# Rolling a matrix by 100 columns: the two DMA rings take blocks from opposite ends instead of sharing each block

## The chip, the cores and the metric

The kernel runs on one core of a Trainium2 chip. The metric is device time in microseconds, the median of several runs; smaller is better. A core has compute engines, of which only GpSimd (POOL in the profile) and VectorE (DVE) do anything here, and 16 DMA engines that move data between the main memory (HBM) and the on-chip memory (SBUF), or from HBM to HBM. Instruction queues of SP, ACT and GpSimd issue the transfers. The transfers of SP and ACT go through one ring each; each transfer is cut into packets that are spread over the 16 DMA engines.

## The reference

x is a matrix of 8192 x 8192 float32 values, 268.44 MB; a row is 32 KiB. The output is x with every row rolled to the right by `shift` = 100 columns:

```python
def reference(x: np.ndarray, shift: int) -> np.ndarray:
    return np.roll(x, shift, axis=1)
```

So output column 100 + i is input column i, and output columns 0 to 99 are input columns 8092 to 8191. There is no arithmetic: 268.44 MB are read and 268.44 MB written.

## The kernel before

With s = 100, the kernel splits the output's columns at a = 128, the next multiple of 128.

Columns 128 to 8191 (the body, 32,256 bytes of each row) are copied from HBM to HBM by line 41, without a stop in SBUF. The rows are grouped in 128 blocks of 64 rows, 2 MiB each. A row's number is 64c + 4e + j, with c the block, e from 0 to 15 and j from 0 to 3. One transfer takes one j of one block: 16 rows, four rows apart, 504 KB. Its 16 rows become 16 packets of 32,256 bytes, one for each DMA engine, and each engine closes with a packet of 4 bytes that counts up the transfer's semaphore. The loop runs over the blocks upwards; j = 0 and j = 2 are issued by SP, j = 1 and j = 3 by ACT (`engines[j % 2]`). So both rings share each block. In the last four blocks each transfer is cut in two at column `mid` = 4096, into 248 KB and 256 KB. Each ring has 264 transfers in all. The Tile framework gives each ring four semaphores in turn, and an issue waits until the transfer that used its semaphore before has landed.

Columns 0 to 127 (the head) come behind this in the program and are GpSimd's: in 16 stages of 512 rows it loads the wrapped columns and the first 28 columns of the rows into SBUF (lines 70, 71 and 74), VectorE copies them together (lines 72 and 75), and line 78 writes them out, 512 bytes a row. These transfers go through GpSimd's own queue (q0 in the profile).

Line 47 and what stands around it (a > 512) isn't reached with this shift. No order is set by hand other than that of the loops, and no body transfer depends on another or on the heads.

Of the kernel before, what the change touches and what calls it, by code (L numbers as in the profile page):

```python
# [1 line left out]

# [4 lines left out]


@with_exitstack
def kernel(  # L10
    ctx: ExitStack,
    tc: tile.TileContext,
    x: bass.AP,
    shift: int,
    out: bass.AP,
):
    nc = tc.nc
    n_rows, n_cols = x.shape
    s = shift % n_cols
    a = -(-s // 128) * 128  # L20
    g = a - s
    P = nc.NUM_PARTITIONS
    engines = [nc.sync, nc.scalar]
    n_chunks = 16
    rows = n_rows // n_chunks

    xm = x.rearrange("(c e j) w -> c j e w", e=16, j=4)
    om = out.rearrange("(c e j) w -> c j e w", e=16, j=4)
    if a < n_cols:
        blocks = n_rows // 64
        mid = (a + n_cols) // 256 * 128
        for c in range(blocks):
            parts = ((a, mid), (mid, n_cols)) if c >= blocks - 4 and a < mid else ((a, n_cols),)
            for j in range(4):
                for lo, hi in parts:  # L40
                    engines[j % 2].dma_start(out=om[c, j, :, lo:hi], in_=xm[c, j, :, lo - s:hi - s])
    if a == 0:
        return


    if a > 512:
        for i in range(n_chunks):
            r = slice(i * rows, (i + 1) * rows)
            nc.gpsimd.dma_start(out=out[r, :s], in_=x[r, n_cols - s:])
            if g > 0:  # L50
                nc.gpsimd.dma_start(out=out[r, s:a], in_=x[r, :g])
        return

    Q = 4
    n_st = n_rows // (P * Q)
    reads = ctx.enter_context(tc.tile_pool(name="reads", bufs=n_st))  # L60
    heads = ctx.enter_context(tc.tile_pool(name="heads", bufs=n_st))
    xt = x.rearrange("(k p q) c -> k p q c", q=Q, p=P)
    ot = out.rearrange("(k p q) c -> k p q c", q=Q, p=P)
    tiles = []
    for k in range(n_st):
        t = reads.tile([P, Q - 1, a], x.dtype)
        h = heads.tile([P, Q, a], x.dtype)
        lead = bass.AP(tensor=x.tensor, offset=(k * P * Q + 1) * n_cols - s,
                       ap=[[Q * n_cols, P], [n_cols, Q - 1], [1, a]])
        nc.gpsimd.dma_start(out=t[:], in_=lead, single_packet=True)  # L70
        nc.gpsimd.dma_start(out=h[:, Q - 1, :s], in_=xt[k, :, Q - 1, n_cols - s:], single_packet=True)  # L71
        nc.vector.tensor_copy(h[:, :Q - 1, :s], t[:, :, :s])  # L72
        if g > 0:
            nc.gpsimd.dma_start(out=h[:, 0, s:], in_=xt[k, :, 0, :g], single_packet=True)  # L74
            nc.vector.tensor_copy(h[:, 1:, s:], t[:, :, s:])  # L75
        tiles.append(h)
    for k, h in enumerate(tiles):
        nc.gpsimd.dma_start(out=ot[k, :, :, :a], in_=h[:], single_packet=True)  # L78


# [1 line left out]
_INS = ['x', 'shift']  # L82
_OUTS = [((8192, 8192), 'float32')]

_NUMBERS = {'shift': 100}


# [26 lines left out]
```

## Time and profile before

| | |
|---|---|
| time, median of 3 runs | 829.13 us (828.62 to 831.27) |
| the profiled execution: its span, first to last instruction | 818.3 us; the page gives no time of its own around the span, and the median lies 10.8 us above it |
| VectorE, GpSimd busy | 7.8 us, 41.1 us |
| the two rings' 31.5 KB packets and completions, share of 16 DMA engines | 48.2% and 46.1% |
| GpSimd's queue | 4.7% |
| moved by all queues | 272.71 MB, mean 333 GB/s |

In the page, a queue's row has its packets, its megabytes and the time that its packets took as a share of the span of 16 engines. GB/s counts each byte that a DMA engine moves once; a copy from HBM to HBM reads and writes it, and so loads HBM twice. The rows of 40 digits or numbers are 40 equal slices of the span, 20.5 us each; a 9 for DMA means that the engines were busy for 90% of the slice or more. A row of DMA issues has the issuing queue, the number of issues, the size of each and the median time from issue to landing.

### The profile page before, as it was taken

How to read it: one execution, taken by the hardware profiler on the slowest of the kernel's cores; microseconds unless marked ns; L12 is line 12 of the kernel's file. 1: busy time of each engine (PE TensorE's matmuls, PEld its weight loads, DVE VectorE, ACT ScalarE, POOL GpSimd, SP SyncE). 2: the span in 40 equal slices, each digit the busy share in tenths (PEclk: the TensorE clock that was granted, in tenths of full speed). 3: DMA queues.
4: the chain of work that ended last, by engine and by line, in shares of the span. 5: the costliest groups of instructions: out<-in, count | busy, mean ns of one | idle time of the engine just before them, and what ended most of it. 6: DMA issues, size and time to landing. Idle time of an engine off the chain costs nothing. (4 is left out here: it accounts for less than half of the span.)

```text
span 818.3 us, 689 instructions
## 1 busy us (share of the span) xinstructions
DVE 7.8 (1%) x32; POOL 41.1 (5%) x68
## 2 busy tenths in 40 slices
DVE  0000000000000000000000000000000000000000
POOL 3011111111010000000000000000000000000000
DMA  9999999999999999999999999999999999999998
GB/s 304 340 344 338 341 334 345 341 346 350 353 352 357 347 332 321 335 328 326 333 330 323 330 331 330 331 326 333 330 328 334 333 330 339 328 333 334 328 318 294
DMA packets 20229, 272.71 MB, mean 333 GB/s; under 512 B 9472, under 2 KB 9728, under 8 KB 11776
## 3 DMA queue, kind: packets, MB, share of 16 engines
q1 hardware_dynamic: 8448, 132.14, 48.2%
q10 hardware_dynamic: 8448, 132.14, 46.1%
q0 software_dynamic: 3328, 8.39, 4.7%
q14 instruction: 5, 0.04, 0.0%
HBM read 268.44 MB, written 268.44 MB: 656 GB/s over the span
## 5 line engine op out<-in xcount | busy, mean ns | idle before, releaser
L78 POOL DMA_DIRECT2D out_dram<-h x16 | 11.4, 712 | 87.2 <-DMA out_dram<-h 51.7
L70 POOL DMA_DIRECT2D t<-in_x_dram x16 | 12.1, 759 | 32.1 <-DMA h<-in_x_dram 31.3
L74 POOL DMA_DIRECT2D h<-in_x_dram x16 | 8.6, 538 | 85.7 <-DMA t<-in_x_dram 85.7
L71 POOL DMA_DIRECT2D h<-in_x_dram x16 | 8.9, 558 | 23.9 <-DMA h<-in_x_dram 23.9
L72 DVE COPY h<-t 128x300 f32<-128x300 f32 x16 | 5.9, 368 | 190.4 <-DMA t<-in_x_dram 190.4
L75 DVE COPY h<-t 128x84 f32<-128x84 f32 x16 | 3.2, 201 | 0.0
L95 POOL MEMSET const-float32-0.0<- 128x1 f32 x1 | 0.1, 99 | 0.2 <-issue 0.2
L95 POOL MEMSET const-bfloat16-1.0<- 128x1 bf16 x1 | 0.1, 101 | 0.0
L95 POOL MEMSET const-uint8-127<- 128x1 uint8 x1 | 0.1, 99 | 0.0
L95 POOL MEMSET const-float32-1.0<- 128x1 f32 x1 | 0.1, 98 | 0.0
## 6 DMA issues: line engine op xcount, KB each, us to landing
out_dram<-in_x_dram ACTq DMA_DIRECT2D x248, 504.0 KB, 12.5
out_dram<-in_x_dram SPq DMA_DIRECT2D x248, 504.0 KB, 12.5
out_dram<-h POOLq DMA_DIRECT2D x16, 256.0 KB, 63.0
t<-in_x_dram POOLq DMA_DIRECT2D x16, 192.0 KB, 32.6
out_dram<-in_x_dram SPq DMA_DIRECT2D x8, 256.0 KB, 5.9
out_dram<-in_x_dram ACTq DMA_DIRECT2D x8, 256.0 KB, 5.8
out_dram<-in_x_dram SPq DMA_DIRECT2D x8, 248.0 KB, 6.1
out_dram<-in_x_dram ACTq DMA_DIRECT2D x8, 248.0 KB, 6.1
```

Of the source, the lines that this page charges most:

```text
L70: nc.gpsimd.dma_start(out=t[:], in_=lead, single_packet=True)
L71: nc.gpsimd.dma_start(out=h[:, Q - 1, :s], in_=xt[k, :, Q - 1, n_cols - s:], single_packet=True)
L72: nc.vector.tensor_copy(h[:, :Q - 1, :s], t[:, :, :s])
L74: nc.gpsimd.dma_start(out=h[:, 0, s:], in_=xt[k, :, 0, :g], single_packet=True)
L75: nc.vector.tensor_copy(h[:, 1:, s:], t[:, :, s:])
L78: nc.gpsimd.dma_start(out=ot[k, :, :, :a], in_=h[:], single_packet=True)
L95: nc = _bacc.Bacc("TRN2", target_bir_lowering=False, num_devices=1)
```

## The change

The loop over the blocks is cut to half its length, and in each pass both rings get a block of their own: SP block c, ACT block 127 - c. Each ring now takes all four j of its block, in order. SP starts at the first block and goes upwards to block 63, ACT starts at the last and goes downwards to block 64. The transfers that are cut in two are those of the last two passes (blocks 62 and 63 for SP, 65 and 64 for ACT). The transfers themselves (rows, columns, sizes, number) are the same as before; which ring issues a transfer, and when, differs. The heads aren't changed.

```diff
         blocks = n_rows // 64
         mid = (a + n_cols) // 256 * 128
-        for c in range(blocks):
-            parts = ((a, mid), (mid, n_cols)) if c >= blocks - 4 and a < mid else ((a, n_cols),)
+        for c in range(blocks // 2):
+            last = c >= blocks // 2 - 2 and a < mid
+            parts = ((a, mid), (mid, n_cols)) if last else ((a, n_cols),)
             for j in range(4):
                 for lo, hi in parts:
-                    engines[j % 2].dma_start(out=om[c, j, :, lo:hi], in_=xm[c, j, :, lo - s:hi - s])
+                    for ring, b in zip(engines, (c, blocks - 1 - c)):
+                        ring.dma_start(out=om[b, j, :, lo:hi], in_=xm[b, j, :, lo - s:hi - s])
     if a == 0:
         return
```

## The prediction

> **What bounds the kernel now.** I read the overview of the page first, then its DMA queues, then the waits of SP's queue, and last the DMA answers for single stretches.
>
> ```profile
> span 818.3 us, 689 instructions
> DVE 7.8 (1%) x32; POOL 41.1 (5%) x68
> DMA  9999999999999999999999999999999999999998
> GB/s 304 340 344 338 341 334 345 341 346 350 353 352 357 347 332 321 335 328 326 333 330 323 330 331 330 331 326 333 330 328 334 333 330 339 328 333 334 328 318 294
> ...
> q1 hardware_dynamic: 8448, 132.14, 48.2%
> q10 hardware_dynamic: 8448, 132.14, 46.1%
> q0 software_dynamic: 3328, 8.39, 4.7%
> ...
> HBM read 268.44 MB, written 268.44 MB: 656 GB/s over the span
> ```
>
> No compute engine matters: VectorE is busy for 1% of the span and GpSimd for 5%. The 16 DMA engines are busy from the first slice to the last, and the three queues' shares add to 99.0%. So time is saved only if a packet gets shorter, and lost only if one gets longer. The page's chain of waits is of no use here: it follows GpSimd's small transfers and ends at 269 us, while the copies run on to 817 us.
>
> The two big queues are the rings of SP (q1) and ACT (q10), told apart by the semaphores of their issues. They move equal bytes in equal packets, and still SP's packets take 2.1% of the span more.
>
> ```profile
> SPq L41 <- DMA out_dram<-in_x_dram: 671.1, 260, 4.8
> ```
> ```profile
> out_dram<-in_x_dram ACTq DMA_DIRECT2D x248, 504.0 KB, 12.5
> out_dram<-in_x_dram SPq DMA_DIRECT2D x248, 504.0 KB, 12.5
> ```
>
> SP waits 671.1 us in 260 waits, each for one of its own earlier copies. It issues 264 copies on four semaphores in turn, so all but the first four wait (264 - 4 = 260): four copies of a ring are in flight, and one lands 12.5 us after its issue. The issuing is far from the limit: 264 issues of 510 ns are 135 us.
>
> The stretch in which nothing but the two rings runs, 290 to 780 us, is the one that the change is priced in:
>
> ```profile
> DMA packets 10073, 161.85 MB, mean 330 GB/s; under 512 B 5030, under 2 KB 5030, under 8 KB 5058
> ...
> q1 hardware_dynamic: 5018, 80.94, 50.5%
> q10 hardware_dynamic: 5013, 80.78, 49.1%
> ```
>
> Half of a queue's packets are 4-byte completions. A 31.5 KB packet of SP therefore takes 0.505 x 490 us x 16 / 2509 = 1.58 us, one of ACT 0.491 x 490 x 16 / 2507 = 1.54 us. The packet records of the trace show two things more. The shortest whole packets take 1.19 us, about a quarter of them do, and the longest twentieth over 2.1 us: an engine can go faster than it mostly goes, so what stretches the packets is the memory behind the engines, or their meeting in it. And most turns of an engine in this stretch read: SP's packet, ACT's packet straight behind it, then the two completions.
>
> Is that memory at a ceiling? A copy counts twice in HBM, GpSimd's transfers to and from SBUF once. By the bytes of the queues that gives, for 2 to 100, 100 to 200, 200 to 290, 290 to 535 and 535 to 780 us, 654, 660, 667, 658 and 663 GB/s. The mixture changes from 15% of GpSimd's small packets to none, and the sum stays within 2%.
>
> **The change, part by part.**
>
> *Counts and sizes: nothing.* Before, 124 blocks of four copies are whole and the last four are cut in two; after, each ring has 62 whole blocks and two cut ones. That is 264 issues a ring both times, 248 of 504 KB and 8 each of 248 and 256 KB, cut at its end. Each copy still has 16 rows, one to each of the 16 packets, spaced four rows (128 KiB) apart. Issues still alternate SP, ACT, so the four semaphores of a ring and its waits stay; what is queued behind a waiting issue is its own ring's next copy, as now. The cut copies' order changes from SP, SP, ACT, ACT to SP, ACT, SP, ACT: at most one issue earlier or later, 0.5 us, hidden by the three copies in flight. With no cover it would be those 0.5 us.
>
> *The end: nothing.* From 780 us on, the engines are 89% busy against 99 to 100% before; the halves drain there on both rings, and will again. If one ring ended ahead of the other its engines would take the other's packets without turns, so no engine would be idle for it.
>
> *GpSimd's and VectorE's work: nothing.* Their instructions come behind the copies in the program, on another queue, and touch columns 0 to 127 alone. All their waits are for their own transfers or VectorE's copies. They end at 269 us of issuing, which leaves 548 us of cover.
>
> *The addresses: the whole question.* Before, an engine's turn takes row 4e + j with SP and the next row, 4e + j + 1, with ACT: neighbours in x and in the output, and both rings are within a block or two (2 MiB each). After, the turn takes row 4e + j of block c with SP, and the same row of block 127 - c with ACT, an odd number of blocks, from 254 MiB down to 2 MiB, away. No row shows such a turn, so it is bounded from both sides by the gap between the two rings, the one place in the trace where equal packets have unequal prices. ACT's packet follows straight behind its lower neighbour and is the cheaper. If all its advantage comes from that neighbour and is lost, ACT's share rises by 2.1% of the span: 0.021 x 818.3 = 17.2 us. If none does, 0. In the other direction, SP's packets could fall to ACT's level when the rings no longer meet in a block: 17.2 us less. In the stretch of the rings alone the gap is 1.4% (50.5 against 49.1), which over the span is 11.5 us; this is the nearest row, as there the turns are undisturbed. But ACT's packet also has no completion ahead of it, which the change leaves, so I count some of the 11.5 to that and take 9 us.
>
> I choose the loss and not the gain because a gain needs room in the memory: the sum of HBM traffic never went above 667 GB/s in five long stretches, 1.7% above the mean of 656, while nothing holds it from below.
>
> *A rule against the change.* The row is the two rings' present spacing: a row or three apart, 656 GB/s in all. The Trainium skill, "DMA: Bandwidth & Descriptors", section "Latency and other measured facts", says that copies between HBM tensors slow down when the streams are a large power of two apart (207 GB/s at a pitch of 512 KiB, 164 at 2 MiB, 103 at 4 MiB), and it offers channel aliasing as an unproven reason. If the spacing of the rings, odd multiples of 2 MiB, cost all that the page gives for 2 MiB, an estimate by it would be 818.3 x 207/164 = 1033 us of span. No run here shows it.
>
> *The sum.* The page gives the span only, 818.3 us; the first instruction fetch in the packet records is 10.5 us ahead of it, together 828.8, against a median of 829.13 of the runs. So span and median agree within 0.4 us, and I count from the median: 829.1 + 0 (counts) + 0 (end) + 0 (GpSimd) + 9 (addresses) = **838 us**, 1.1% more.
>
> **The rivals.**
>
> *Nothing changes (829 us).* The memory is at its ceiling and doesn't care for order. For it speaks the sum of 654 to 667 GB/s under very different mixtures. Against it: a quarter of the packets run at 1.19 us and others at nearly twice that, so a packet does depend on what it meets, and a result within 0.3% (2.5 us, about what a measurement of this kernel can tell from no change) would need the meetings to cost exactly the same.
>
> *Faster: the rings stop meeting (812 us).* Two streams in one block of 2 MiB may meet more often in one part of the memory than streams in two distant ones. If SP's packets then cost what ACT's do, 17.2 us go: 812 us. The best slice of the late stretch, 339 GB/s against the mean of 330, gives 818.3 x (1 - 330/339) = 22 us: 807 us, the lower bound. It decides as soon as the late sum passes 667 GB/s. Against it: the best long stretch is 667.
>
> *Clearly slower: equal places collide (852 us and more).* SP's and ACT's packets in a turn, and all the engines' that are in step, stand at equal distances from the start of their blocks. If places equal but for whole blocks share a part of the memory, ACT's read starts where SP's write still drains. The lowest late slice of whole packets, 321 GB/s, is the nearest row: 818.3 x (330/321 - 1) = 23 us, 852; with both rings' packets dearer by 2.1% it is 34 us, 863. For it speaks the long tail of packets over 2.1 us, which shows that meetings happen; against it, that in the present order, too, a copy's write stands opposite its own read, 16 pairs at any time, and the sum is still 656. The page's rule named above would be this rival's cause.
>
> **How the numbers follow.** My forecast, slower by 0.3 to 2.5%, gets 0.42; clearly slower 0.17; no change 0.15; faster 0.26. Slower is thus 0.59, same 0.15, faster 0.26. The forecast alone would lie between 832 and 849. As cases of both signs hold much of the chance, the range takes the bounds of both: 807 us, with some 0.06 below it, and 863, with some 0.12 above it.
>
> **What the profile after will show.** The queues' packets and bytes must be the same, the 264 issues a ring and 12 to 13 us to landing too, and the engines' shares must still add to about 99%. If I am right, q10's share rises to at least q1's, and the stretch from 290 to 780 us moves about 326 GB/s. If shares of both rings rise together, it is the collision. If both fall and the stretch passes 333 GB/s, memory had room, and the ceiling was one of the old order alone. If the engines' shares add to clearly less than 99%, I have missed a wait. I would be wrong above all if the ceiling that I read from five stretches is no property of the memory but of the two rings' nearness, which all five have in common.

## The result: 0.35% slower, and the profile after

The changed kernel takes 832.51 us (828.60 to 836.06 in 22 runs) beside 829.68 us of the kernel before (826.53 to 831.27). The ratio is 1.0035, with a 95% interval from 1.0023 to 1.0047: a loss of 2 to 4 us, where 9 were forecast.

The page after, in the lines that answer to those of before (the overview, the DMA rates, the queues and the HBM traffic):

```profile
span 829.3 us, 689 instructions
DVE 7.8 (1%) x32; POOL 41.1 (5%) x68
...
GB/s 301 350 328 338 340 334 344 334 343 347 346 335 354 326 329 328 325 333 325 325 328 325 333 327 314 327 333 321 328 325 325 323 327 333 328 327 335 319 302 287
...
q1 hardware_dynamic: 8448, 132.14, 47.1%
q10 hardware_dynamic: 8448, 132.14, 46.7%
q0 software_dynamic: 3328, 8.39, 5.0%
...
HBM read 268.44 MB, written 268.44 MB: 647 GB/s over the span
```

Its DMA issues, and what SP's queue waited for (total us, times, longest):

```profile
out_dram<-in_x_dram ACTq DMA_DIRECT2D x248, 504.0 KB, 12.8
out_dram<-in_x_dram SPq DMA_DIRECT2D x248, 504.0 KB, 12.8
```
```profile
SPq L38 <- DMA out_dram<-in_x_dram: 681.7, 260, 5.3
```

And its stretch from 290 to 780 us:

```profile
DMA packets 9993, 160.20 MB, mean 327 GB/s; under 512 B 4976, under 2 KB 4976, under 8 KB 5033
...
q10 hardware_dynamic: 4958, 79.97, 49.9%
q1 hardware_dynamic: 4958, 79.97, 49.5%
```

Packets, bytes, waits and issues are the same in number, and the three queues still fill 98.8% of the 16 engines. So nothing waits that didn't wait before; each packet takes a little longer. The 327 GB/s of this stretch can't be set against the 330 of the page before, though.

The two pages may not be subtracted. The profiled execution of the change took 831.04 us with a span of 829.3, and in all later profiles, too, the time is 1.8 us above the span. The first page, 818.3 us, so belongs to an execution of about 820 us, faster than any of the 22 runs of before (826.53 at least). In the experiments, the unchanged kernel takes 818.25 us on one chip and 829.3 to 829.9 us on three others: the first page reads as one of a faster chip. The 11.0 us between the pages' spans are therefore mostly chip and not change. That the late stretch came out at 327 GB/s where 326 were forecast, with q10's share above q1's there, proves nothing either: experiment 5 shows the kernel before with 328 GB/s and q10 ahead on a chip of like speed. Each experiment below is compared with the kernel before on its own chip: a number like 1.0022 is its time divided by that of the kernel before, with the 95% interval behind it.

### The profile page after: what moved, and what is told of

Its sections match the earlier page's. It is cut to its first block, busy times and chain, and to the rows that moved or that the text cites. A ratio compares the mean times of both kernels' runs of the same rounds, so it can differ in the third digit from the quotient of the medians.

```text
span 829.3 us, 689 instructions
## 1 busy us (share of the span) xinstructions
DVE 7.8 (1%) x32; POOL 41.1 (5%) x68
```

## The experiments

To follow them, write an engine's packets in their order. A turn is SP's packet, then ACT's, and then comes the next turn. With each row named by its place j in its block:

- before: SP 0, ACT 1, SP 2, ACT 3, and so on, in one block
- the change: SP 0, ACT 0, SP 1, ACT 1, and so on, with ACT in a far block, at the same place as SP

Four theories could explain a loss: the *neighbour* (a turn no longer takes two adjacent rows, which is my forecast), the *distance* of the two regions, the *equal place* (two rows in a turn that lie at the same place of their 2 MiB blocks collide), and the *direction* (ACT goes downwards).

**1. Even and odd blocks, both upwards.** Near, equal places, no neighbours.

```diff
-                    for ring, b in zip(engines, (c, blocks - 1 - c)):
+                    for ring, b in zip(engines, (2 * c, 2 * c + 1)):
```

> SP takes the even blocks and ACT the odd ones, both upwards, so the rings stay 2 MiB apart at equal places of their blocks. Neighbour theory (an engine's turn on row r and r + 1 is what the change loses): 1.0035 of the time before, as in the change. Distance theory (two far regions cost): 1.000, since the rings are next to each other. Equal-place theory (rows equal but for whole blocks collide): 1.0035 or more. Direction theory (ACT going downwards costs): 1.000.

Measured: 1.0022 (1.0009 to 1.0035). Slower with the rings only 2 MiB apart and without a descending ring: against the distance and the direction as the whole cause.

**2. Two halves of the matrix, both upwards.** Far, equal places, no neighbours, nothing descends.

```diff
-                    for ring, b in zip(engines, (c, blocks - 1 - c)):
+                    for ring, b in zip(engines, (c, blocks // 2 + c)):
```

> SP takes blocks 0 to 63 and ACT blocks 64 to 127, both upwards: always 128 MiB apart at equal places. Neighbour: 1.0035. Distance: 1.0035. Equal place: 1.0035, and more if a larger power of two aliases more. Direction: 1.000.

Measured: 1.0030 (1.0018 to 1.0042). The direction is out. The constant 128 MiB cost no more than the change's odd multiples of 2 MiB.

**3. The change with ACT two rows on.** Everything as in the change but the equal place.

```diff
-                    for ring, b in zip(engines, (c, blocks - 1 - c)):
-                        ring.dma_start(out=om[b, j, :, lo:hi], in_=xm[b, j, :, lo - s:hi - s])
+                    for ring, (b, i) in zip(engines, ((c, j), (blocks - 1 - c, (j + 2) % 4))):
+                        ring.dma_start(out=om[b, i, :, lo:hi], in_=xm[b, i, :, lo - s:hi - s])
```

> As the change, but ACT takes the rows of a block in the order j = 2, 3, 0, 1, so that a turn's two rows are 64 KiB off the equal place. Neighbour: 1.0035. Distance: 1.0035. Equal place: 1.000. Direction: 1.0035.

Measured: 0.9970 (0.9958 to 0.9982). The loss is gone, although the blocks are as far apart, ACT goes downwards, and no turn has neighbours. Of the four theories only the equal place is left.

**4. Shared blocks without neighbours.** As before, but SP takes j = 0, 1 and ACT j = 2, 3 of each block.

```diff
-                    for ring, b in zip(engines, (c, blocks - 1 - c)):
-                        ring.dma_start(out=om[b, j, :, lo:hi], in_=xm[b, j, :, lo - s:hi - s])
+                    for ring, (b, i) in zip(engines, ((2 * c + j // 2, j % 2), (2 * c + j // 2, 2 + j % 2))):
+                        ring.dma_start(out=om[b, i, :, lo:hi], in_=xm[b, i, :, lo - s:hi - s])
```

> Both rings share each block upwards as before, but SP takes j = 0, 1 and ACT j = 2, 3, so that a turn's rows are two apart and no longer neighbours. Neighbour: 1.0035. Distance, equal place and direction: 1.000.

Measured: 0.9996 (0.9986 to 1.0007). Adjacent rows in a turn are worth nothing that can be measured. My forecast's cause falls here. The queues on this kernel's page say the same: without any neighbours in a turn, ACT's packets are still the cheaper ones, by 2.2% of the span.

```profile
q1 hardware_dynamic: 8448, 132.14, 48.2%
q10 hardware_dynamic: 8448, 132.14, 46.0%
```

**5. and 6. The kernel before and the change on one chip.**

> The kernel before once more, to have its profile from the same chip as the next three. All theories: 1.000; its span within 2 us of its time, if the 10.8 us that I found between the first page's span and the median of the runs were a matter of two chips.

> The change itself, on the same chip as the two kernels that follow. All theories: 1.0035.

Measured: the kernel before 1.0015 (0.9999 to 1.0030) against itself, which shows how far a ratio of this kind can stray; the change 1.0049 (1.0031 to 1.0067). The profiled execution of the former took 827.95 us with a span of 826.2, that of the change 834.28 us with 832.5; the first is below the median of its runs and the second above, so this pair of pages shows the difference too large (6 us in place of 4).

On this chip, the queues of the kernel before, over the span and then from 290 to 780 us:

```profile
q1 hardware_dynamic: 8448, 132.14, 47.5%
q10 hardware_dynamic: 8448, 132.14, 47.0%
```
```profile
DMA packets 10012, 160.74 MB, mean 328 GB/s; under 512 B 4992, under 2 KB 4992, under 8 KB 5033
...
q10 hardware_dynamic: 4977, 80.30, 50.0%
q1 hardware_dynamic: 4979, 80.26, 49.7%
```

The same stretch of the change on this chip:

```profile
DMA packets 9895, 159.11 MB, mean 325 GB/s; under 512 B 4930, under 2 KB 4930, under 8 KB 4966
...
q10 hardware_dynamic: 4925, 79.52, 49.8%
q1 hardware_dynamic: 4921, 79.42, 49.8%
```

Two readings. SP's packets, dearer by 2.1% of the span in the first page, are here dearer by 0.5% of it, and in the late stretch slightly cheaper (49.7 against 50.0), with the same program. And in this pair both rings' packets are dearer with the change: with half of a queue's packets whole, SP's go from 0.497 x 490 us x 16 / 2490 = 1.57 us to 0.498 x 490 x 16 / 2461 = 1.59, ACT's from 1.58 to 1.59. It isn't one ring's advantage that is lost.

**7. Even and odd blocks, ACT two rows on.**

```diff
-                    for ring, b in zip(engines, (c, blocks - 1 - c)):
-                        ring.dma_start(out=om[b, j, :, lo:hi], in_=xm[b, j, :, lo - s:hi - s])
+                    for ring, (b, i) in zip(engines, ((2 * c, j), (2 * c + 1, (j + 2) % 4))):
+                        ring.dma_start(out=om[b, i, :, lo:hi], in_=xm[b, i, :, lo - s:hi - s])
```

> Even and odd blocks, both upwards, with ACT's rows in the order j = 2, 3, 0, 1. Equal-place theory: the 1.0022 of the even and odd blocks at equal places is gone, 1.000 or less. If distance also brings a gain (what would explain 0.997 with the ends and 1.000 with the shared block): 1.000, as the rings are near each other. If the gain is that of each ring taking all four rows of a block in order: 0.997.

Measured: 1.0006 (0.9995 to 1.0017). The 1.0022 of experiment 1 went when the equal place went. That each ring takes a block's four rows in order brings no gain.

**8. The change with ACT one row on.** As experiment 3, with `(j + 1) % 4`.

> As the change, with ACT's rows in the order j = 1, 2, 3, 0, so that a turn's rows are one row (32 KiB) off the equal place. Equal-place theory, with any other place good enough: 0.997 as with two rows. If the offset matters and only two rows are good: 1.000 to 1.0035.

Measured: 1.0022 (1.0009 to 1.0035). This went against the simple theory: the places within a turn differ, and the loss stays. Written out, the order offers an explanation: SP 0, ACT 1, SP 1, ACT 2, SP 2. Now ACT's row and the *next* turn's row of SP are at equal places. The collision would have moved from one hand-over of the engine to the other.

**9. and 10. Two rows on, again with the ends, and with the two halves.** The first is the kernel of experiment 3, the second is experiment 2 with `(blocks // 2 + c, (j + 2) % 4)` for ACT.

> The change with ACT's rows in the order j = 2, 3, 0, 1 once more, on this call's chip. If its gain is its own: 0.997 again. If the gain was the chip's, and the equal place is all that the change costs: 1.000.

> SP takes blocks 0 to 63 and ACT blocks 64 to 127, both upwards, ACT's rows in the order j = 2, 3, 0, 1. Equal-place theory: the 1.0030 of the same kernel without the other order goes, to 1.000 or less. Distance theory: 1.003 stays.

Measured: 0.9986 (0.9971 to 1.0000) and 1.0008 (0.9995 to 1.0021). The loss of experiment 2 is gone as well. The ends with two rows on came out 0.14 and 0.3% faster in the two tries, on two chips; that is at the edge of what can be told, and the halves of the matrix don't have it.

**11. and 12. The effect made large.** All 16 rows of a transfer 64 rows apart, so that all engines stand at equal places of different blocks; and 65 rows apart as a control. The rings take adjacent rows in turn, upwards.

```diff
-        for c in range(blocks // 2):
...
+        first, done = 0, 0
+        for pitch, groups in ((64, 8),):   # the control: ((65, 7), (57, 1))
+            for k in range(groups):
+                xg = x[first:first + 16 * pitch].rearrange("(e t) w -> t e w", e=16)
+                og = out[first:first + 16 * pitch].rearrange("(e t) w -> t e w", e=16)
+                for t in range(pitch):
+                    parts = ((a, mid), (mid, n_cols)) if done >= 4 * blocks - 16 else ((a, n_cols),)
+                    for lo, hi in parts:
+                        engines[done % 2].dma_start(out=og[t, :, lo:hi], in_=xg[t, :, lo - s:hi - s])
+                    done += 1
+                first += 16 * pitch
```

> The effect made large: the 16 rows of every transfer are 64 rows (2 MiB) apart in place of 4, so that all 16 engines read and write at equal places but for whole blocks; the rings take neighbouring rows in turn, upwards, as before. Equal-place theory: clearly slower than before, over 1.02, since 15 pairs and not one collide. If only the two rows of one engine's turn matter: 1.00.

> The control of the one before: the 16 rows of a transfer are 65 rows (2 MiB and 32 KiB) apart, in the last 912 rows 57; all else as there. Equal-place theory: much of the loss of 64 rows goes, nearer to 1.00. If a wide spread itself costs: as with 64 rows.

Measured: with 64 rows 1348.52 us against 829.94, 1.62 times as long; the four runs scatter from 1240.86 to 1466.60 us, 1.50 to 1.77 times, so the size is rough. With 65 rows 856.50 us, 1.0339 (1.0314 to 1.0363). The page of the 64 rows, its rates, queues and traffic:

```profile
GB/s 209 238 209 204 237 259 218 222 203 218 221 204 212 195 203 201 193 188 192 206 170 195 207 185 189 194 198 210 195 197 184 205 198 194 189 192 190 199 185 160
...
q10 hardware_dynamic: 8448, 132.14, 51.2%
q1 hardware_dynamic: 8448, 132.14, 45.0%
q0 software_dynamic: 3328, 8.39, 2.9%
...
HBM read 268.44 MB, written 268.44 MB: 397 GB/s over the span
```

and of the 65 rows:

```profile
HBM read 268.44 MB, written 268.44 MB: 629 GB/s over the span
```

The engines are as full as ever (99.1%), with the same packets and bytes; each packet only takes longer. The change with two rows on (experiment 9) moves 650 GB/s over its span on this chip; 253 of them are lost with 64 rows, and 32 KiB more between the rows bring back 232. So most of the loss comes with the equal places, and not with the spread as such. The control isn't free of equal places, though: in two successive transfers, the row of ACT's that goes to one engine (65e + t + 1) lies exactly 64 rows before the row of SP's that goes to the next (65e + 65 + t). Whether its own 3.4% are such meetings between engines, or the spread, no run decides.

**13. The change with ACT three rows on.** As experiment 3, with `(j + 3) % 4`.

> As the change, with ACT's rows in the order j = 3, 0, 1, 2. In an engine's turns the order of rows is then SP j, ACT j - 1, SP j + 1, so no two packets in a row stand at equal places, neither from SP to ACT nor from ACT to SP. With an offset of one row the second of these is equal, with none the first, with two neither. Hand-over theory: 0.997 to 1.000, as with two rows. If a row at an odd distance is what costs: 1.002, as with one row.

Measured: 0.9997 (0.9982 to 1.0013). An odd offset, as in experiment 8, but neither hand-over has equal places, and there is no loss. This is what the hand-over theory said and the other didn't.

**14. and 15. Two and eight engines at one place.** Experiment 11 with rows 8 apart, `((8, 64),)`, and 32 apart, `((32, 16),)`.

> The 16 rows of a transfer are 8 rows (256 KiB) apart, so that engines e and e + 8 are 2 MiB apart, at equal places: each engine's row has one partner in the same transfer in place of none, 8 pairs in all. If the price is in proportion to the partners (62% for 15): 1.04. If two at a place is what the memory takes at no cost: 1.00.

> The 16 rows of a transfer are 32 rows (1 MiB) apart, so that the engines stand at two places of the 2 MiB blocks, eight at each: seven partners. In proportion to the partners: 1.29. If equality modulo 2 MiB is not the measure but modulo 1 MiB: 1.6, as with 64 rows; modulo 4 MiB or more: less than half of 1.29's loss.

Measured: 1.0023 (1.0005 to 1.0040) and 1.3350 (1.3266 to 1.3434). The second ratio is that of the two shorter of four runs; all four lie between 1100.24 and 1146.77 us, 1.33 to 1.38 times the time before. The late stretch of the 32 rows, on its chip:

```profile
DMA packets 7832, 117.13 MB, mean 239 GB/s; under 512 B 3708, under 2 KB 3708, under 8 KB 4272
```

Counted by places in 2 MiB blocks, the price isn't in proportion to the partners from the first one on: one costs 0.2% (hardly more than the 0.15% by which the kernel before strayed from itself, and with an interval from 0.05 to 0.4), seven about 34%, fifteen about 62%. The estimate of 4% for one partner was far too high, that of 29% for seven nearly right. If places counted by 1 MiB blocks alone, 32 rows would have cost as much as 64, and they don't. That 2 MiB is the memory's own measure isn't shown by this; rows 16 apart were not run.

## Why the prediction was wrong, and where it was right

All the changed body orders with rows 4 apart, by whether an engine's successive packets meet at equal places (the kernel before, against which they are measured, has no such meeting):

| order of an engine's rows | equal at a hand-over | ratio |
|---|---|---|
| the change: 0 / 0, 1 / 1 | SP to ACT | 1.0035, 1.0049 |
| even and odd blocks | SP to ACT | 1.0022 |
| two halves | SP to ACT | 1.0030 |
| ends, one on: 0 / 1, 1 / 2 | ACT to SP | 1.0022 |
| ends, two on: 0 / 2, 1 / 3 | none | 0.9970, 0.9986 |
| ends, three on: 0 / 3, 1 / 0 | none | 0.9997 |
| two halves, two on | none | 1.0008 |
| even and odd, two on | none | 1.0006 |
| shared blocks, 0, 1 and 2, 3 | none | 0.9996 |

The five results with an equal hand-over have a mean of 1.0032, the six without one of 0.9994. The difference is 0.38% or 3.1 us; an engine makes 264 turns, so that is some 12 ns for a turn of 3.1 us. Single ratios of this size mean little, as the kernel before strayed to 1.0015 against itself; the two groups don't overlap.

*Counts, end, GpSimd: nothing.* Right. Packets, bytes, 260 waits and the shares' sum stayed.

*The addresses as the whole question, and that they cost.* The addresses are all that differs, and the sign was right. It rested on a ceiling, which no order went clearly past; but what was to be lost, the neighbour, is worth nothing, and that something else cost a little was luck.

*The price of the addresses, 9 us.* This step failed, in its cause and in its size. It took most of the gap between SP's and ACT's packets in the late stretch, 1.4% on the first page, for what a neighbouring row is worth. The same program on another chip has the opposite gap there, 0.3% in SP's favour (0.5% in ACT's favour over the span), and the order without neighbours has the gap all the same (2.2% over the span): the neighbour doesn't make it, and what does, the chip or the single execution, stays open. And the neighbour is worth nothing (0.9996 without it). What stands in its place is the equal place of successive packets, 3 us.

*The rival "nothing changes".* Its 2.5 us were nearly met: the medians differ by 2.8 us. Its reason, a memory that doesn't care for order, is not: experiment 11 moves the same bytes in 1.5 to 1.8 times the time.

*The rival "equal places collide".* It named the equal place as the cause, and priced it at 23 us from the worst slice and 34 us from the ring gap. The condition holds, and the price was too high by a factor of eight or more. The way it gave, SP's write still draining when ACT's read starts, is not shown. The engines of one transfer are never at equal places in the change, as their rows are 128 KiB apart in a block of 2 MiB; only the two packets that follow each other on one engine are. That they meet where one hands over to the other fits all eleven ratios of the table, above all the ends with one and with three rows on, but no row of a trace shows an overlap: it stays inferred. It also supposes that both rings give row e of a transfer to the same engine, which the packet records don't name. And one other way stays open. In the records of the change, about half of the busy engines hold an SP packet at any moment and half an ACT packet (7.9 each in the mean of the late stretch). If places that agree modulo less than 2 MiB (128 KiB, say, the spacing of a transfer's rows) cost a little as well, which no run excludes, rows of two engines would meet too, in the same orders of the table, and the collision could lie between engines.

*The rule of the Trainium skill.* "DMA: Bandwidth & Descriptors", section "Latency and other measured facts", has copies slow down at large powers of two of row pitch and get back to speed with a few KiB more. The runs agree where the pitch is that of the rows of one transfer: about 1.62 at 2 MiB (1.50 to 1.77), more than the 207/164 = 1.26 by the figures of the Trainium skill, about 1.34 at 1 MiB, and 1.03 with 32 KiB added. The rule spoke in the right direction, too, but the estimate of 1033 us by it took the spacing of the two rings for that pitch, and this spacing costs 0.2 to 0.5%.

*The rival "faster".* Two rings in distant blocks gain nothing by that: without the equal place, the halves are at 1.0008 and the ends with three rows on at 0.9997. What the 0.14 to 0.3% of the ends with two rows on are, if they are real, stays open.

*The ceiling.* I took 654 to 667 GB/s for a limit below which the order could only cost. No order went clearly past it, and the best, the ends with two on, reached 659 GB/s over its span against 656 and 657 of the shared blocks on pages of like speed. Whether this is the memory's own limit no run here decides.

*Span and median.* That instruction fetches explain the 10.8 us between them was wrong: in the later profiles, too, they begin 10.3 to 10.7 us ahead of the span, and still the time is only 1.8 us above it. The rest reads as another chip. It left the sum unhurt, as that counted from the median of the runs.

## What to carry to other kernels

When two queues feed the same DMA engines, write down the order of addresses that one engine sees, and look at each packet beside the next, in both directions. Here an offset of two or three rows (of four) cost nothing and took the loss away, while an offset of one only moved the equal place to the next hand-over. Keep the rows that the engines of one transfer handle at the same time off multiples of 1 or 2 MiB; this is the large effect (about 34 and 62%), and the order of the rings the small one. Don't price an effect by a gap between two queues in a single profile, before the same program has shown that gap twice.

## What the runs showed of the hardware that was not expected

- The price of rows at equal places of 2 MiB blocks rises steeply: two of 16 engines at one place 0.2%, at the edge of what can be told, eight about 34%, sixteen about 62%, with engines about 99% busy each time.
- Rows 2 MiB and 32 KiB apart still cost 3.4% against rows 128 KiB apart (here neighbouring engines' rows of the two rings meet at equal places).
- Far regions cost nothing by themselves: halves of a matrix of 268 MB, two rows on, run at 1.0008.
- The same kernel takes 818 us on one chip and 829 to 830 on three others, 1.4% apart, four times the effect under study.
- Which ring's packets are dearer is no property of a ring: with one and the same kernel, SP's are dearer by 2.1% of the span in the first page and by 0.5% in a later one, on another chip; with the even and odd blocks, it is ACT's by 2.4%:

```profile
q10 hardware_dynamic: 8448, 132.14, 48.1%
q1 hardware_dynamic: 8448, 132.14, 45.7%
```
